# First tile of x in two banks, first norm weights in a tile of their own, two turns of attention probabilities later, last output block in half banks

## The chip, the cores and the metric

The kernel runs on one core of one Trainium2 chip. The metric is the device time of one execution in microseconds (us), the median of several runs. TensorE is called PE here, VectorE DVE, ScalarE ACT, GpSimd POOL and SyncE SP. PSUM is the memory that PE writes its results to, in banks of 512 float32 columns on 128 partitions, and SBUF is the memory that holds all other tiles.

## What is computed

Two layers on x of 512 tokens by 1024 columns, float32. Each layer is, cut to what matters:

```python
h = rmsnorm(x, norm_mix)
z = h @ w_in                      # q, k, v of attention, q, k, v, o and gates of the mLSTM, two branch gates
att = sliding_window_attention(q_a, k_a, v_a, att_sinks)
hm = sigmoid(o_m) * rmsnorm(mlstm_chunkwise(q_m, k_m, v_m, i_pre, f_pre))
mixed = sigmoid(g_a) * (att @ w_att_branch) + sigmoid(g_m) * (hm @ w_m_branch)
x = x + mixed @ w_out
u = relu(rmsnorm(x, norm_ffn) @ w_ff1)
x = x + (u * u) @ w_ff2
```

Attention has 8 query heads on 2 key heads and works on blocks of 128 queries, each of which sees its own block and the one before.

## The kernel before

x stays in SBUF for the whole program, in four tiles `xtok[t][j]` of 2 x 128 tokens by 512 columns. A product needs columns of x as rows, so PE turns x in pieces of 128 columns (`Norm.transposes`, four 128x128 transposes into one bank), and ACT and DVE scale the piece by the norm weight and split it into a high part and a rest (`Norm.turn`, `split`). Weights are loaded by SP, 512 columns at a time, and split in the same way (`chunk`): ACT writes the high part `wh`, DVE the rest `wl`. Each product of a 128-row piece is then three matmuls (`mm3`, line 203): high by high, high by rest, rest by high. Every one of them is recorded on line 47, and every transpose on line 52.

**The order of the work** is written by hand. `weave` (line 255) takes a list of steps with widths (0.25 is one `mm3` group), and puts side jobs between them at the places that numbers name. On each engine the instructions then stand in one fixed order, and an instruction waits for the semaphores of what it reads and of what last used its buffer. PSUM is given out in turn: the three banks of the tag `aux` go round, so the fourth request waits until the readers of the first are done.

**The start** (lines 357 to 399). SP and ACT each ask for one half of the first 128 columns of x (line 373), ACT then for the first 256 norm weights as a column (`gain0`, line 380), for all weights of both layers as rows (`grow`, line 381) and for its half of the next 128 columns of x. PE runs dummy matmuls on ones until data is there, turns the first piece of x into one bank (`x0`, line 393), turns `grow` (line 395), runs three more dummy matmuls (line 398), and begins with the products of the first piece: four with `wh` and the high part, four with `wl`, four with the rest. The four differ in the 128 tokens that they take from the turned piece. Between the first two fours stands the turn of the second piece of x. `turn_first` (line 310) has ACT make the high part of the first piece (line 313), and DVE makes its rest between the first two weight splits (lines 172 to 178, 316). The turned norm weights are copied to `gcol` by DVE (line 175), and the pieces of x from the third on are scaled by `gcol`.

**Attention** is woven into the gate products of each layer. There are eight units (128 queries, one key head), numbered i = 0 to 7. For each, lines 936 to 943 place the scores (`att_scores`, two banks of aux), the softmax, the turn of the probabilities (`att_probs`: PE transposes into aux, ACT and DVE split it, POOL masks it) and the product with the values (`att_out`, one bank of aux, read by ACT line 744 and DVE line 748). `turn_at` on line 938 says when the probabilities are turned.

**The end.** The second product of the MLP of the last layer ends with slot 4 of its last part (`product`, line 1619, with `which` = "aux"). It adds up 256 tokens by 512 columns in two banks of aux, in two halves h of two 128-row pieces each; in h = 1 the first block's products stand before those of the second. `gain` (line 1316) has DVE scale each block and add it to x (line 1327), the last block in two halves of 256 columns, and SP and ACT write them out (line 1330).

Of the kernel before, what the change touches and what calls it, by code (L numbers as in the profile page):

```python
# [8 lines left out]
F32 = mybir.dt.float32  # L9
# [4 lines left out]
ALU = mybir.AluOpType  # L14
# [19 lines left out]
def hybrid_kernel(ctx, tc, x, norm_mix, w_in, att_q_norm, att_k_norm, att_sinks, m_gate_bias,  # L34
# [69 lines left out]
    def f32(ap):  # L104
        return ap.bitcast(F32)
# [16 lines left out]
    neg = const.tile([MH, P], F32, name="neg")  # L122
    gp.memset(neg, NEG)
    grow = const.tile([24, P], F32, name="grow")
    gcol = const.tile([P, 40], F32, name="gcol")

    first_gains = []

    def gains(row, c0, held=False):
        n = row.shape[0]  # L130
        gps = aux([P, n])
        pe.transpose(gps, row, ident[:n, :n])
        if held:
            first_gains.append((gcol[:, c0:c0 + n], gps))
        else:
            ve.tensor_copy(gcol[:, c0:c0 + n], gps)

    def g_mix(l, k):
        return gcol[:, 8 * l + k:8 * l + k + 1]
# [10 lines left out]
    def chunk(src, behind=()):  # L150

        with tc.high_priority():
            raw = now["wraw"].tile([P, T], F32, tag="w", name=nm("w"))
            off = 0
            for s in src:
                n = s.shape[1]
                if first_loads:

                    n0 = {0: 0, 1: 2}.get(chunks[0], len(first_loads) - 1)
                    with tc.issue_after(first_loads[n0].ins):  # L160
                        first_weights.append(nc.sync.dma_start(raw[:, off:off + n], s))
                    chunks[0] += 1
                    if chunks[0] == 8:
                        first_loads.clear()
                else:
                    asked[0] = nc.sync.dma_start(raw[:, off:off + n], s)
                off += n
        with tc.high_priority(lead[0]):
            wh = now["wsp"].tile([P, T], F32R, tag="wh", name=nm("wh"))
            wl = now["wsp"].tile([P, T], F32R, tag="wl", name=nm("wl"))  # L170
            n = chunks[0] - 1 if first_loads else KT
            if n == 0 and first_rest:
                made = ve.tensor_copy(wh[:, :off], raw[:, :off])
                for then in (lambda: ve.tensor_tensor(wl[:, :off], raw[:, :off], f32(wh[:, :off]), op=ALU.subtract),
                             first_rest.pop(), lambda: ve.tensor_copy(*first_gains.pop())):
                    with tc.issue_after(made.ins):
                        made = then()
                return wh, wl
            with ExitStack() as order:
                for i in behind:  # L180
                    order.enter_context(tc.issue_after(i.ins))
                if n < KT:

                    order.enter_context(tc.issue_after(norm0.hi[max(n - 1, 0)].ins))
                    order.enter_context(tc.issue_after(norm0.lo[max(n - 1, 0)].ins))
                sc.activation(wh[:, :off], raw[:, :off], AF.Copy)  # L186
                ve.tensor_tensor(wl[:, :off], raw[:, :off], f32(wh[:, :off]), op=ALU.subtract)  # L187
        return wh, wl
# [90 lines left out]
    class Norm:  # L279
# [30 lines left out]
        def turn_first(self, ps):  # L310
            self.groups[0] = [inp.tile([P, 4, T], F32R, tag=t, name=nm("i")) for t in ("ih", "il")]
            h, lo = self.acts[0] = [g[:, 0, :] for g in self.groups[0]]
            self.hi[0] = last_split[0] = sc.activation(h, ps, AF.Copy, scale=self.gain(0))

            def rest():
                self.lo[0] = last_split[1] = made = ve.scalar_tensor_tensor(lo, ps, self.gain(0), f32(h), op0=ALU.mult,
                                                                            op1=ALU.subtract)
                return made

            first_rest.append(rest)  # L320

# [55 lines left out]
    with tc.high_priority():  # L377
        load_x(0, 1, 0, nc.sync)
        load_x(0, 1, 1, nc.scalar)
        nc.scalar.dma_start(gain0, norm_mix[0, 0:2 * P].rearrange("(k p) -> p k", p=P))  # L380
        nc.scalar.dma_start(grow[0:16, :], norm_mix.rearrange("l (k p) -> (l k) p", p=P))
# [61 lines left out]
    def mixer(l, norm, late, order, phase):  # L443
# [791 lines left out]
    def mlp(l, norm, phase):  # L1235
# [80 lines left out]
        def gain(t, j, ps, done=False, last=False):  # L1316

            with tc.high_priority():  # L1320
                for i in range(2):
                    b = 2 * t + i
                    xh = xtok[t][j][:, i, :]

                    for c in ((0, H), (H, T)) if done and last and b == NB - 1 else ((0, T),):
                        cc = slice(*c)
                        ve.scalar_tensor_tensor(xh[:, cc], ps[i][:, cc], ms[j][:, b:b + 1], xh[:, cc],  # L1327
                                                op0=ALU.mult, op1=ALU.add)
                        if done and final:
                            (nc.scalar if c[0] else nc.sync).dma_start(  # L1330
                                out[0, b * P:(b + 1) * P, j * T + c[0]:j * T + c[1]], xh[:, cc])
# [287 lines left out]
        def product(which, fresh, w, sources, gains, seeds=None):  # L1619
# [12 lines left out]

            def run(h):
                if h == 0 and fresh:
                    pairs[which] = [aux(), aux()] if which == "aux" else two_banks(which)
                ps, (hi, lo), (ah, al) = pairs[which], ws[h], a[0]
                at = [(kt, i) for kt in range(2 * h, 2 * h + 2) for i in range(2)]

                for kt, i in sorted(at, key=lambda e: e[1]) if h else at:
                    c = slice(i * P, (i + 1) * P)  # L1640
                    mm3(ps[i], ah[:, kt, c], al[:, kt, c], hi[:, kt % 2, :], lo[:, kt % 2, :],
                        fresh and kt == 0, False, skip_group_check=True)

            def done():
                for t, j, d in gains:
                    gain(t, j, pairs[which], d, which == "aux")
# [241 lines left out]
```

## Time and profile before

| what | value |
|---|---|
| median of 3 runs | 1263.53 us (1263.24 to 1263.57) |
| the profiled execution's own time | 1263.76 us |
| span of that execution, first to last instruction | 1262.1 us |
| what lies around the span | 1.66 us |
| busy time of PE, DVE, ACT, POOL | 1255.6, 1034.8, 813.3, 283.2 us |
| mean granted clock of PE | 1.000 |

A profile row of the timeline reads: start in us, length in us, engine, line, operation, tile written <- tiles read, shape, how many of a kind in a row, and in brackets how long the engine had been idle and what ended that. "ACTq" or "SPq" is the queue of an engine that issues a transfer. A matmul's length holds its way through the array, which overlaps the next one: 512 columns are shown as 0.39 us long, and the starts of two in a row lie about 0.23 us apart. The time that a matmul takes is therefore read from the distance of the starts.

### The profile page before, as it was taken

To read this page: it belongs to the slowest core of one execution; us is meant where nothing else is said; L and a number is where in the kernel's file an instruction comes from. 1 tells how busy PE (TensorE), PEld (TensorE's weight loads), DVE (VectorE), ACT (ScalarE), POOL (GpSimd) and SP (SyncE) were. 2 spreads that over 40 slices of the span, in tenths; PEclk is the share of its full clock that TensorE was granted. 3 is DMA by queue.
4 is the path that set the end of the run, shared out by engine and by line. 5 is a ranking of instruction groups with operands and counts; after the bars stand their busy time and mean duration, and the time that the engine had idled before them with its cause. 6 is when DMAs were issued, how large, how long until landed. Compare 5 with 4: busy or idle time off the path is not lost.

```text
span 1262.1 us, 19896 instructions
## 1 busy us (share of the span) xinstructions
PE 1255.6 (99%) x7170; PEld 1098.8 (87%) x7170; DVE 1034.8 (82%) x1645; ACT 813.3 (64%) x1442; POOL 283.2 (22%) x373
## 2 busy tenths in 40 slices
PE   9999999999999999999999999999999999999998
PEld 7888888888999899999888888888889999999987
DVE  5788988688998877878857989876889978778787
ACT  5578578645785665656554885876467766556563
POOL 4514131021122021031115042310303211311300
PEclk9999999999999999999999999999999999999999
DMA  5424573468899889997224354634779988998953
GB/s 159 114 69 134 127 130 93 142 137 212 179 250 182 233 170 211 235 187 190 36 75 118 89 137 110 117 111 132 156 208 189 240 191 228 171 223 207 201 134 100
DMA packets 145538, 199.68 MB, mean 158 GB/s; under 512 B 11032, under 2 KB 85632, under 8 KB 145440
## 3 DMA queue, kind: packets, MB, share of 16 engines
q0 software_dynamic: 50432, 68.30, 33.9%
q1 hardware_dynamic: 94016, 129.72, 33.5%
q8 instruction: 56, 0.92, 0.3%
q10 hardware_dynamic: 992, 0.40, 0.1%
q14 instruction: 42, 0.34, 0.1%
HBM read 195.24 MB, written 2.10 MB: 156 GB/s over the span
## 4 chain that ended last, share of the span: by engine, by line
PE 99%; DMA 0%; ACTq 0%; DVE 0%; issue 0%; DVEq 0%
PE mm L47 84%; PE aux L47 13%; PE aux L52 3%; DMA grow<-in_norm_mix_dram 0%; ACTq L373 0%; ACTq L380 0%; DVE x L1327 0%; DVEq L1884 0%
## 5 line engine op out<-in xcount | busy, mean ns | idle before, releaser
L1263 ACT ACTIVATE wh<-raw 128x1024 fp32r<-128x1024 f32 x224 | 235.0, 1055 | 149.9 <-PE mm L47 75.9
L1264 DVE TENSOR_TENSOR wl<-raw,wh 128x1024 fp32r<-128x1024 f32 x224 | 271.3, 1221 | 73.5 <-ACT wh L1263 70.7
L47 PE MATMUL mm<-i,wh 128*128 128x256 f32 (+1 forms) x1344 | 331.1, 339 | 0.0
L47 PEld LDWEIGHTS mm<-i,wh 128*128 128x128 f32 x1344 | 223.8, 190 | 19.4
L47 PE MATMUL mm<-i,wl 128*128 128x256 f32 (+1 forms) x672 | 224.7, 335 | 0.0
L47 PE MATMUL mm<-wh,uh 128*128 128x512 f32 x440 | 172.1, 391 | 0.0
L47 PE MATMUL mm<-wl,uh 128*128 128x512 f32 x440 | 171.7, 390 | 0.0
L47 PE MATMUL mm<-wh,ul 128*128 128x512 f32 x440 | 171.3, 389 | 0.0
L1425 POOL DMA_DIRECT2D raw<-in_w_ff_dram x56 | 72.5, 1375 | 349.3 <-DVE wl L1264 85.4
L47 PEld LDWEIGHTS mm<-i,wl 128*128 128x128 f32 x672 | 127.4, 190 | 13.5
L186 ACT ACTIVATE wh<-w 128x512 fp32r<-128x512 f32 (+1 forms) x143 | 85.3, 603 | 60.9 <-PE mm L47 44.0
L187 DVE TENSOR_TENSOR wl<-w,wh 128x512 fp32r<-128x512 f32 (+1 forms) x143 | 95.5, 671 | 34.8 <-ACT wh L186 34.0
L47 PE MATMUL mm<-t,wh 128*128 128x256 f32 x576 | 104.5, 283 | 0.0
L47 PE MATMUL mm<-wh,i 128*128 128x512 f32 (+1 forms) x352 | 99.5, 357 | 0.0
L47 PEld LDWEIGHTS mm<-wh,ul 128*128 128x128 f32 x440 | 82.6, 188 | 17.5
L47 PEld LDWEIGHTS mm<-wh,uh 128*128 128x128 f32 x440 | 82.8, 188 | 16.2
L47 PEld LDWEIGHTS mm<-wl,uh 128*128 128x128 f32 x440 | 82.8, 188 | 15.5
L47 PEld LDWEIGHTS mm<-t,wh 128*128 128x128 f32 x576 | 90.7, 192 | 1.3
L1674 POOL DMA_DIRECT2D raw<-in_w_ff_dram x40 | 48.4, 1214 | 169.8 <-DVE wl L1264 120.7
L47 PE MATMUL mm<-t,wl 128*128 128x256 f32 x288 | 81.5, 283 | 0.0
L1327 DVE SCALAR_TENSOR_TENSOR x<-mm,ms,x 128x512 f32<-128x512 f32 x102 | 72.4, 745 | 10.7 <-PE mm L47 10.4
L47 PEld LDWEIGHTS mm<-wh,i 128*128 128x128 f32 x352 | 62.0, 188 | 8.6
(336 smaller groups left out, 2536.6 us busy)
## 6 DMA issues: line engine op xcount, KB each, us to landing
raw<-in_w_ff_dram SPq DMA_DIRECT2D x144, 512.0 KB, 6.0
raw<-in_w_ff_dram POOLq DMA_DIRECT2D x96, 512.0 KB, 7.8
w<-in_w_in_dram SPq DMA_DIRECT2D x112, 256.0 KB, 2.8
a<-in_w_in_dram POOLq DMA_DIRECT2D x32, 256.0 KB, 5.7
qa<-in_w_out_dram POOLq DMA_DIRECT2D x12, 512.0 KB, 6.0
a<-in_w_in_dram SPq DMA_DIRECT2D x16, 256.0 KB, 4.4
w<-in_w_att_branch_dram SPq DMA_DIRECT2D x16, 256.0 KB, 3.1
w<-in_w_m_branch_dram SPq DMA_DIRECT2D x16, 256.0 KB, 2.7
```

What stands on the lines that cost most here:

```text
L47: latest[0] = nc.tensor.matmul(*args, **kw)
L52: latest[0] = nc.tensor.transpose(*args)
L186: sc.activation(wh[:, :off], raw[:, :off], AF.Copy)
L187: ve.tensor_tensor(wl[:, :off], raw[:, :off], f32(wh[:, :off]), op=ALU.subtract)
L1263: last_high[0] = sc.activation(hi, src, AF.Copy)
L1264: last_rest[0] = ve.tensor_tensor(lo, src, f32(hi), op=ALU.subtract)
L1327: ve.scalar_tensor_tensor(xh[:, cc], ps[i][:, cc], ms[j][:, b:b + 1], xh[:, cc], op0=ALU.mult, op1=ALU.add)
L1425: return gp.dma_start(to[h], src(h, i, j), accum_op=ALU.add)
L1674: gp.dma_start(to[h], src(h, i, j), accum_op=ALU.add)
```

## The change

It has four parts, and nothing else in the order of the engines moves.

1. The first turned piece of x goes to two aux tiles of 256 columns, each for two blocks of tokens. ACT makes the high part in two instructions and DVE the rest in two.
2. The rows of `norm_mix` go to a tile of their own, `grow0`, and are turned later: `gains_behind` places the transpose behind the products with `wl`, and DVE copies the result to `gcol` at once, where before the copy was held back for a place of its own. One dummy matmul stands ahead of the products, where there were three.
3. The turn of the probabilities moves by 0.25 for unit 4 (from +0.25 to +0.5) and for unit 5 (from 0 to +0.25), in both layers.
4. The last output block is added up in two tiles of 256 columns, half a bank of aux and half of the pair "y". Each of its 12 matmuls of 512 columns becomes two of 256, in h = 1 all of the first half ahead of the second.

```diff
+    grow0 = const.tile([16, P], F32, name="grow0")
...
-                made = ve.tensor_copy(wh[:, :off], raw[:, :off])
-                for then in (lambda: ve.tensor_tensor(wl[:, :off], raw[:, :off], f32(wh[:, :off]), op=ALU.subtract),
-                             first_rest.pop(), lambda: ve.tensor_copy(*first_gains.pop())):
-                    with tc.issue_after(made.ins):
-                        made = then()
+                high = ve.tensor_copy(wh[:, :off], raw[:, :off])
+                with tc.issue_after(high.ins):
+                    low = ve.tensor_tensor(wl[:, :off], raw[:, :off], f32(wh[:, :off]), op=ALU.subtract)
+                with tc.issue_after(low.ins):
+                    first_rest.pop()()
...
+            cs = [slice(2 * P * t, 2 * P * (t + 1)) for t in range(2)]
+            for c, ps in zip(cs, halves):
+                self.hi[0] = last_split[0] = sc.activation(h[:, c], ps, AF.Copy, scale=self.gain(0))
...
-            x0 = norm.transposes(0)
-        with tc.issue_after(latest[0].ins):
-            gains(grow[0:16, :], 0, True)
-        with tc.issue_after(latest[0].ins):
-            for _ in range(3):
-                pe.matmul(idle[:, :P], ones, ones, start=True, stop=True)
+            x0 = [aux((P, 2 * P)) for _ in range(2)]
+            for b in range(NB):
+                pe.transpose(x0[b // 2][:, b % 2 * P:(b % 2 + 1) * P], xtok[b // 2][0][:, b % 2, 0:P], ident)
+        with tc.issue_after(latest[0].ins):
+            pe.matmul(idle[:, :P], ones, ones, start=True, stop=True)
...
-            turn_at = at + 3.45 + (0.25 if i == 4 else 0)
+            turn_at = at + 3.45 + {4: 0.5, 5: 0.25}.get(i, 0)
...
-                    pairs[which] = [aux(), aux()] if which == "aux" else two_banks(which)
+                    pairs[which] = ([aux(), [aux((P, H)), banks("y")[:, 0, :H]]] if which == "aux"
+                                    else two_banks(which))
...
-    late = ([(max(0.25, k - 0.85), lambda k=k: turn_behind(norm, k)) for k in range(1, KT)]
+    late = ([(0.6, gains_behind)] + [(max(0.25, k - 0.85), lambda k=k: turn_behind(norm, k)) for k in range(1, KT)]
```

On PE at the start of the program, before the change (`x_0` are the two tiles that hold the first columns of x, `i` the split pieces of x, `aux` the banks that go round):

```order
L52 MATMUL aux_105<-ident,x_0_86 128x128 x2
L52 MATMUL aux_105<-ident,x_0_88 128x128 x2
L52 MATMUL aux_110<-ident,grow 128x16
L47 MATMUL aux_101<-ones 128x128 x3
L47 MATMUL mm_178<-wh_184,i_115 128x512
L47 MATMUL mm_179<-wh_184,i_115 128x512
L47 MATMUL mm_180<-wh_184,i_115 128x512
L47 MATMUL mm_181<-wh_184,i_115 128x512
L52 MATMUL aux_194<-ident,x_0_86 128x128 x2
L52 MATMUL aux_194<-ident,x_0_88 128x128 x2
L47 MATMUL mm_178<-wl_185,i_115 128x512
```

The same place after the change, from the last dummy matmul to the first product with the rest of the first piece:

```order
L47 MATMUL aux_102<-ones 128x128
L47 MATMUL mm_177<-wh_183,i_113 128x512
L47 MATMUL mm_178<-wh_183,i_113 128x512
L47 MATMUL mm_179<-wh_183,i_113 128x512
L47 MATMUL mm_180<-wh_183,i_113 128x512
L52 MATMUL aux_193<-ident,x_0_87 128x128 x2
L52 MATMUL aux_193<-ident,x_0_89 128x128 x2
L47 MATMUL mm_177<-wl_184,i_113 128x512
L47 MATMUL mm_178<-wl_184,i_113 128x512
L47 MATMUL mm_179<-wl_184,i_113 128x512
L47 MATMUL mm_180<-wl_184,i_113 128x512
L52 MATMUL aux_204<-ident,grow_84 128x16
```

The turn of the norm weights has moved from ahead of the first product to behind the eighth; the turn of the second piece of x stands where it stood.

On DVE at the start, after the change, from the rest of the first piece to that of the third (`gcol` are the turned norm weights):

```order
L315 SCALAR_TENSOR_TENSOR i_114<-aux_106,gain_1_91,i_113 128x256
L315 SCALAR_TENSOR_TENSOR i_114<-aux_107,gain_1_91,i_113 128x256
L183 TENSOR_TENSOR wl_214<-w_211,wh_213 128x512
L196 SCALAR_TENSOR_TENSOR i_114<-aux_193,gain_1_91,i_113 128x512
L183 TENSOR_TENSOR wl_239<-w_236,wh_238 128x512
L132 COPY gcol<-aux_204 128x16
L196 SCALAR_TENSOR_TENSOR i_114<-aux_220,gcol,i_113 128x512
```

The copy to `gcol` stood behind the first `wl` of this list before, and now stands behind the second, directly ahead of the third piece of x, whose scale it is.

On PE in the attention of the first layer, after the change (`kT,tq` are scores, `ident,t` turns of probabilities, `t,v` products with the values, all in aux; the rows of gate products between them are left out where "..." stands):

```order
L47 MATMUL aux_1417<-kT_637,tq_647 128x256 x4
...
L52 MATMUL aux_1430<-ident,t_1205 128x128 x4
L47 MATMUL aux_1445<-t_1318,v_116_639 128x512
...
L47 MATMUL aux_1474<-kT_637,tq_647 128x256 x4
...
L47 MATMUL aux_1502<-kT_637,tq_647 128x256 x4
L52 MATMUL aux_1509<-ident,t_1302 128x128 x4
```

Unit 4's turn (`t_1205`) stood one group of three gate products earlier and now stands directly ahead of unit 3's product with the values; unit 5's turn (`t_1302`) stood ahead of the last scores of this list and now stands behind them, so it takes the next bank in the round, the one that holds unit 3's product with the values.

More of the change, by code (lines that the diff above doesn't have):

```diff
@@ L132, in gains @@
         pe.transpose(gps, row, ident[:n, :n])
[L133 to L136, printed above, removed]
+        ve.tensor_copy(gcol[:, c0:c0 + n], gps)
     def g_mix(l, k):
@@ L308, in turn, with turn_first @@
             self.hi[k], self.lo[k] = last_split
-        def turn_first(self, ps):
+        def turn_first(self, halves):
             self.groups[0] = [inp.tile([P, 4, T], F32R, tag=t, name=nm("i")) for t in ("ih", "il")]
             h, lo = self.acts[0] = [g[:, 0, :] for g in self.groups[0]]
-            self.hi[0] = last_split[0] = sc.activation(h, ps, AF.Copy, scale=self.gain(0))
+            cs = [slice(2 * P * t, 2 * P * (t + 1)) for t in range(2)]
+            for c, ps in zip(cs, halves):
+                self.hi[0] = last_split[0] = sc.activation(h[:, c], ps, AF.Copy, scale=self.gain(0))
             def rest():
-                self.lo[0] = last_split[1] = made = ve.scalar_tensor_tensor(lo, ps, self.gain(0), f32(h), op0=ALU.mult,
-                                                                            op1=ALU.subtract)
-                return made
+                for c, ps in zip(cs, halves):
+                    self.lo[0] = last_split[1] = ve.scalar_tensor_tensor(lo[:, c], ps, self.gain(0), f32(h[:, c]),
+                                                                         op0=ALU.mult, op1=ALU.subtract)
             first_rest.append(rest)
@@ L1314, in neither, with gain @@
                 ve.scalar_tensor_tensor(d, p, -1.0, q, op0=ALU.mult, op1=ALU.subtract)
-        def gain(t, j, ps, done=False, last=False):
+        def gain(t, j, ps, done=False):
             with tc.high_priority():
@@ L1323, in gain @@
                     xh = xtok[t][j][:, i, :]
[L1325 removed]
+                    halved = isinstance(ps[i], list)
+                    for c in ((0, H), (H, T)) if halved else ((0, T),):
                         cc = slice(*c)
[L1327 to L1328 removed]
+                        ve.scalar_tensor_tensor(xh[:, cc], ps[i][c[0] // H] if halved else ps[i], ms[j][:, b:b + 1],
+                                                xh[:, cc], op0=ALU.mult, op1=ALU.add)
                         if done and final:
@@ L1645, in done @@
                 for t, j, d in gains:
-                    gain(t, j, pairs[which], d, which == "aux")
+                    gain(t, j, pairs[which], d)
                 if seeds:
```

15 lines of the change are left out of this document (9 added, 6 removed).

## Prediction

> **What bounds the kernel now.** The first page says that PE is busy nearly throughout:
>
> ```profile
> PE 1255.6 (99%) x7170; PEld 1098.8 (87%) x7170; DVE 1034.8 (82%) x1645; ACT 813.3 (64%) x1442; POOL 283.2 (22%) x373
> ```
>
> The waits of PE name two places, and the second is one that the change touches:
>
> ```profile
> PE aux L47 <- POOL ones L114: 1.2, 1, 1.2
> PE aux L52 <- DMA grow<-in_norm_mix_dram: 0.8, 1, 0.8
> ```
>
> So all that an edit can win is distance between matmuls that is longer than it need be: 1262.1 - 1255.6 = 6.5 us idle, 2.0 of them in these two waits, and what hides inside "busy". I therefore read the timeline at the places of the change. A change of 0.2% (2.5 us) is about what a measurement of this kernel can tell from none.
>
> The start on PE, then on ACT with its queue, then the transfers that were asked for there:
>
> ```profile
> 3.94 1.03 PE L52 MATMUL aux<-ident,x 128*128 128x128 f32 x4
> 5.96 0.94 PE L47 MATMUL aux<-ones 128*128 128x128 f32 x6
> 6.65 1.18 PE L47 MATMUL mm<-wh,i 128*128 128x512 f32 x4
> 7.67 0.60 PE L52 MATMUL aux<-ident,x 128*128 128x128 f32 x4
> 8.02 1.18 PE L47 MATMUL mm<-wl,i 128*128 128x512 f32 x4
> ```
>
> ```profile
> 1.35 0.49 ACTq L380 DMA_DIRECT2D gain<-in_norm_mix_dram  x1
> 2.39 0.45 ACTq L373 DMA_DIRECT2D x<-in_x_dram  x1
> 5.01 0.69 ACT L313 ACTIVATE i<-aux,gain 128x512 fp32r<-128x512 f32 x1 [0.86 <-PE aux L52]
> ```
>
> ```profile
> gain<-in_norm_mix_dram ACTq DMA_DIRECT2D x1, 1.0 KB, 3.5
> x<-in_x_dram ACTq DMA_DIRECT2D x1, 128.0 KB, 4.8
> ```
>
> ACT has the high part at 5.01 + 0.69 = 5.70, but PE sits behind `grow` and the dummies until 6.65. That is the wait that goes. What is late next is in the last row: half of the second piece of x, asked for at 2.39, lands at 2.39 + 4.8 = 7.19. Today its transposes start at 7.67 and never meet it.
>
> **Part 1 and 2, the start.** The scale lands at 1.35 + 3.5 = 4.85, so ACT's first half of the high part runs from about 4.9 to 5.3 and the second to about 5.75; two halves are no faster than one whole, but the products of the first two token blocks can begin at about 5.4. Four products take 7.67 - 6.65 = 1.02, so they end at about 6.4. Then the second pair of transposes waits for 7.19. Whatever the bank split brings forward, this wait takes back: with one whole tile the products would run from 5.75 to 6.8 and wait for the same 7.19, so I cost the split itself at nothing. Its extra instructions on ACT and DVE lie in the idle time before the second weights.
>
> Today the products with `wl` start 8.02 - 7.67 = 0.35 after the first of four transposes, half of which, 0.17, belongs to the second pair. So they start at 7.19 + 0.17 = 7.36 instead of 8.02: 0.66 earlier. Then comes the turn of the norm weights, which used to lie in the wait. Its price is read from the other turn of this kind, later on PE:
>
> ```profile
> 27.33 0.40 PE L47 MATMUL mm<-wl,i 128*128 128x512 f32 x1
> 27.56 0.40 PE L47 MATMUL mm<-wh,i 128*128 128x512 f32 x1
> 27.89 0.24 PE L52 MATMUL aux<-ident,grow 24*128 24x24 f32 x1
> ...
> 28.39 0.40 PE L47 MATMUL mm<-wl,i 128*128 128x512 f32 x1
> ```
>
> From 27.56 to 28.39 are 0.83, where two products alone take 2 x 0.23: the turn costs 0.37. Left over at the start: 0.66 - 0.37 = **0.29**. Its low end is nothing or a loss of 0.1, if the piece of x lands 0.3 to 0.4 later than here; its high end is set by the next thing that could be late, the third piece:
>
> ```profile
> 8.30 0.17 DVE L175 COPY gcol<-aux 128x16 f32<-128x16 f32 x1
> 10.59 0.69 DVE L187 TENSOR_TENSOR wl<-w,wh 128x512 fp32r<-128x512 f32 x1 [0.81 <-ACT wh L186]
> 11.29 0.69 ACT L199 ACTIVATE i<-aux,gcol 128x512 fp32r<-128x512 f32 x1 [0.73 <-DVE wl L187]
> 12.01 0.75 DVE L200 SCALAR_TENSOR_TENSOR i<-aux,gcol,i 128x512 fp32r<-128x512 f32 x1 [0.73 <-ACT i L199]
> 13.61 0.39 PE L47 MATMUL mm<-wh,i 128*128 128x512 f32 x1
> ```
>
> The copy to `gcol` now stands on DVE behind the `wl` that ends at 11.28, and ACT's 11.29 waits for it: both move by 0.2, and the rest of the third piece, which ended at 12.76, ends at 12.96. PE reads it first at 13.61, so 0.6 is the most that the start can win. With 0.29 the cover holds. Behind DVE's copy stand that rest and the next `wl`, each 0.2 later, and their readers have the same cover.
>
> **Part 3, the turns of probabilities.** In each layer one turn starts late: 0.50 after the matmul before it, where the next turn in the same layer starts 0.23 after.
>
> ```profile
> 104.61 0.39 PE L47 MATMUL mm<-i,wl 128*128 128x512 f32 x1
> 105.11 0.63 PE L52 MATMUL aux<-ident,t 128*128 128x128 f32 x4
> 109.30 0.64 PE L47 MATMUL aux<-kT,tq 128*128 128x256 f32 x4
> 109.77 0.63 PE L47 MATMUL mm<-i,wh 128*128 128x512 f32 x2
> 110.24 0.39 PE L47 MATMUL mm<-i,wl 128*128 128x512 f32 x1
> 110.47 0.63 PE L52 MATMUL aux<-ident,t 128*128 128x128 f32 x4
> 729.81 0.39 PE L47 MATMUL mm<-i,wl 128*128 128x512 f32 x1
> 730.31 0.63 PE L52 MATMUL aux<-ident,t 128*128 128x128 f32 x4
> ```
>
> ```profile
> 103.51 0.69 DVE L716 TENSOR_TENSOR t<-t,den 128x512 f32<-128x512 f32 x1
> 104.12 0.84 DVE L748 TENSOR_TENSOR t<-aux,t 64x256 f32<-64x256 f32 x2
> 110.25 0.84 DVE L748 TENSOR_TENSOR t<-aux,t 64x256 f32<-64x256 f32 x2
> ```
>
> Unit 4's probabilities are ready at 104.20, so what PE waits for is its bank: DVE leaves unit 2's product with the values at 104.96, 0.15 before the turn starts. One group of three products later (0.70 from 109.77 to 110.47) PE comes at 105.11 - 0.27 + 0.70 = 105.54 and finds it free. That gives 0.27 per layer, **0.54** in both.
>
> Unit 5 pays with a new wait. Its turn now takes the bank of unit 3's product with the values, which DVE leaves at 111.09, usable at 111.24. PE gets there at 109.03 (109.30 - 0.27), plus 0.47 for those scores, two groups at 0.70 and 0.47 for the last scores: 111.37. The cover is 0.13. If it is gone, up to 0.27 per layer comes back; the range of this part is 0 to 0.54. The later masks on POOL and the later splits are read by products with the values some 2 us later, and cost nothing.
>
> **Part 4, the last block.** Products of 512 and of 256 columns, 24 and 48 in a row, from the chain, then the end on PE, DVE and ACT's queue, and a single 256-wide addition from the groups:
>
> ```profile
> 1163.66 5.47 PE mm L47 x24
> 1169.13 5.75 PE aux L47 x48
> ```
>
> ```profile
> 1257.48 0.39 PE L47 MATMUL aux<-wh,ul 128*128 128x512 f32 x1
> 1257.90 0.88 DVE L1327 SCALAR_TENSOR_TENSOR x<-aux,ms,x 128x256 f32<-128x256 f32 x2 [0.61 <-PE aux L47]
> 1258.81 0.37 ACTq L1330 DMA_DIRECT2D out_dram<-x  x1
> ```
>
> ```profile
> L1362 DVE SCALAR_TENSOR_TENSOR x<-aux,gcol,x 128x256 f32<-128x256 f32 x8 | 3.6, 477 | 0.0
> ```
>
> 12 products at 5.47/24 = 0.228 become 24 at 5.75/48 = 0.120: 2.88 - 2.74 = 0.14 more. In return the first half is complete 6 x 0.12 = 0.72 before the end, longer than the 0.48 that DVE needs for it, and only one addition follows the last matmul: 0.88 - 0.48 = 0.40 less. Net **0.26** earlier for ACT's output, which is the last to be asked for; between 0.1 (if the two halves' transfers get in each other's way) and 0.35.
>
> The Trainium skill speaks against this part ("Perfetto Trace Analysis", Optimizing Tensor Performance: larger matmuls are the more efficient), and its formula for the spacing ("TensorE: Matmul & The Clock Gate", Back-to-back issue gap) has 2.5 ns for each matmul more; by that, an estimate, the halving would cost 12 x 2.5 ns = 0.03 instead of 0.14; the rows here show the larger price, and the sum goes by them.
>
> **The sum.** 0.29 + 0.54 + 0.26 = 1.09 us earlier. The profiled execution's own time is 1263.76 (span 1262.1 and 1.66 around it), which would become 1262.67; it lies 0.23 above the median of 1263.53, so for the median I say **1262.4**.
>
> **The rivals.**
> 1. *The wait for x takes the place of the wait for `grow`, in full.* If the second piece lands at 7.48 or later, the start wins nothing: 1262.7. For it: the row is one transfer among several in flight. Against: today's runs agree within 0.33.
> 2. *Unit 5's wait takes the place of unit 4's.* A cover of 0.13 is gone if DVE's chain to 111.09 is no faster than here while PE is earlier: 0 instead of 0.54, time 1263.0.
> 3. *Slower: PE's clock stays low for longer.* Four transposes take 1.03 at 3.94 and 0.60 at 7.67, and the dummies at 5.96 lie between: PE begins at about half speed and has sped up by 7.67. The change removes dummies and puts two holes (about 0.35 and 0.8 us) into the first 7 us. If the slow phase then lasted to the end of the first twelve products, the eight after 7.19 would take 0.23 more each and the transposes 0.43 more: 2.3 lost, with 0.8 won in parts 3 and 4 and 0.29 at the start, time 1264.7. It decides at whether the products at 7.36 stand 0.23 or 0.46 apart. Against: today a hole of 0.8 at the same place does no harm, and real products start earlier than the dummies did. The Trainium skill ("TensorE: Matmul & The Clock Gate", Part 1) has the clock rise after a busy window of about 3.4 us and fall only after an idle one; by that rule no hole here is long enough.
> 4. *More.* If x lands earlier, the start wins up to 0.6: 1262.1.
>
> That the edits don't do what they say is excluded for the order of the engines; that the two-bank tile by itself moves nothing is part of the forecast.
>
> **How the numbers follow.** Forecast 0.62, rival 1 0.12, rival 2 0.12, rival 3 0.06, rival 4 0.08. The range takes in the low ends of parts 1 to 4 and rivals 1, 2 and 4, with the runs' spread of 0.3 at both ends: 1261.8 to 1263.4. No case but an unnamed one passes 2.5 us either way: even all parts at their best give 0.6 + 0.54 + 0.35 = 1.5. So faster by over 0.2% 0.02, within 0.95, slower 0.03.
>
> **What would show it.** Right: the first product at about 5.4, the second transposes split by a wait until 7.2, the `wl` products from 7.36 and those of the second piece 0.3 earlier than before; unit 4's and 5's turns 0.23 behind the matmul before them in both layers; one addition of 0.48 behind the last matmul. Wrong: a turn with 0.4 or more ahead of it; products 0.46 apart behind 7 us; a hole ahead of the third piece's products at about 12.8; an end that is not 0.26 nearer to the last matmul.

## The result and the profile after

| kernel | runs | median (us) | lowest to highest |
|---|---|---|---|
| before | 17 | 1263.82 | 1263.24 to 1265.86 |
| after | 17 | 1266.40 | 1265.00 to 1269.96 |
| before, on a later chip | 15 | 1265.22 | 1263.34 to 1265.98 |
| after, on that chip | 11 | 1264.70 | 1263.26 to 1268.46 |

The ratio is 1.0018 [1.0011, 1.0026] in the first set and 1.0001 [0.9992, 1.0010] in the second. So the change cost 2.6 us or nothing, and did not win the 1.1 us that I forecast: 1266.4 lies outside my range (1261.8 to 1263.4).

The runs of before fall into two groups. Of 125 in five sets, 65 lie between 1262.99 and 1264.36 and 60 between 1264.74 and 1266.24; the three that I saw ahead of the prediction were all of the lower group. What parts them, by the profiles below, is how soon PE's clock rises at the start, so single profiles are compared here by places and not by their end.

The profiled execution of after took 1268.20 (span 1266.5) and is one of the longest. The first line of its page says that PE's busy time has grown by 1.8 us, so that most of the 4.4 us of span are not in PE's work:

```profile
PE 1257.4 (99%) x7178; PEld 1098.6 (87%) x7178; DVE 1033.1 (82%) x1646; ACT 813.1 (64%) x1443; POOL 284.5 (22%) x373
```

All waits of PE in it (waited for; us in total, times, longest):

```profile
PE mm L47 <- ACT wh L182: 2.0, 2, 1.6
PE aux L47 <- POOL ones L114: 1.2, 1, 1.2
PE mm L47 <- ACT i L311: 0.6, 1, 0.6
PE mm L47 <- ACT kvi L463: 0.6, 1, 0.6
PE mm L47 <- DVE wl L183: 0.5, 2, 0.2
```

The wait for `grow` is gone. New at the start is a wait of the first product for ACT's high part (`i`). The other new ones are for weight splits (`wh`, `wl`) and for `kvi` (a product that ACT copies out of PSUM), and none of them is at a place that the change touches.

**The three places of the change.** The start and the third piece of x, on PE:

```profile
3.94 0.66 PE L52 MATMUL aux<-ident,x 128*128 128x128 f32 x4
...
5.42 1.20 PE L47 MATMUL mm<-wh,i 128*128 128x512 f32 x4 [0.60 <-ACT i L311]
6.46 0.88 PE L52 MATMUL aux<-ident,x 128*128 128x128 f32 x4
7.09 1.17 PE L47 MATMUL mm<-wl,i 128*128 128x512 f32 x4
8.20 0.23 PE L52 MATMUL aux<-ident,grow 16*128 16x16 f32 x1
...
13.31 0.51 PE L47 MATMUL mm<-wh,i 128*128 128x512 f32 x1
13.65 0.60 PE L52 MATMUL aux<-ident,x 128*128 128x128 f32 x4
```

The first product stands at 5.42 (6.65 before), the `wl` products at 7.09 (8.02 before), the next transposes at 13.65 (13.85 before): 0.20 won. The turns of units 4 and 5 in the first layer, each with the row ahead of it:

```profile
106.06 0.40 PE L47 MATMUL mm<-i,wl 128*128 128x512 f32 x1
106.29 0.60 PE L52 MATMUL aux<-ident,t 128*128 128x128 f32 x4
...
111.60 0.63 PE L47 MATMUL aux<-kT,tq 128*128 128x256 f32 x4
112.20 0.63 PE L52 MATMUL aux<-ident,t 128*128 128x128 f32 x4
```

Unit 4's turn starts 0.23 behind the matmul ahead of it (0.50 before). Unit 5's stands behind four scores, which take 4 x 0.12 = 0.48, and starts 0.60 after the first of them: it waits 0.12. The end:

```profile
1262.42 0.28 PE L47 MATMUL mm<-wh,ul 128*128 128x256 f32 x1
1262.74 0.48 DVE L1325 SCALAR_TENSOR_TENSOR x<-mm,ms,x 128x256 f32<-128x256 f32 x1 [0.23 <-PE mm L47]
1263.26 0.37 ACTq L1328 DMA_DIRECT2D out_dram<-x  x1
```

One addition of 0.48 follows the last matmul, as forecast.

**Where the time went.** The same matmul can be found in both timelines; the difference of its two starts says how far PE is behind before at that place (13.65 - 13.85 = -0.20). It changes at these places only:

| place in after (us) | what happens there | PE behind before, from then on |
|---|---|---|
| 0 to 14 | the start | -0.20 |
| 44.5 | wait for `kvi`, whose ACT stood behind a late weight split | +0.67 |
| 84 | a chance wait of a turn | +0.75 |
| 106 to 112 | turns of units 4 and 5 | +0.53 |
| 149 to 150 | wait for DVE, weights late since 142 | +1.12 |
| 170 to 172 | wait for `wh`, then `wl` | +2.48 |
| 733 to 739 | turns of units 4 and 5 | +2.25 |
| 797 to 800 | wait for `wh`, then `wl` | +4.77 |
| 870 | a chance wait that before had | +4.66 |
| end | last block | +4.44 |

The places of the change won 0.20 + 0.22 + 0.23 + 0.22 = 0.87 together; the four other waits lost 0.87 + 0.59 + 1.36 + 2.52 = 5.3. The first of them, on ACT and on PE:

```profile
43.79 1.31 ACT L182 ACTIVATE wh<-w 128x512 fp32r<-128x512 f32 x2 [2.25 <-DMA w<-in_w_in_dram]
45.01 1.58 ACT L463 ACTIVATE kvi<-mm,ncol 128x264 f32<-128x264 f32 x4
45.52 0.74 PE L47 MATMUL mm<-i,wh 128*128 128x512 f32 x2 [0.60 <-ACT kvi L463]
```

In before the same copies of ACT stand at 44.27 and PE does not wait for them:

```profile
44.27 1.58 ACT L466 ACTIVATE kvi<-mm,ncol 128x264 f32<-128x264 f32 x4
```

The largest, on ACT and on PE:

```profile
798.15 0.63 ACT L182 ACTIVATE wh<-w 128x512 fp32r<-128x512 f32 x1 [4.29 <-DMA w<-in_w_in_dram]
798.83 0.50 PE L47 MATMUL mm<-wh,i 128*128 128x512 f32 x1 [1.61 <-ACT wh L182]
```

ACT stood idle for 4.29 us until a weight load landed, and PE for the split behind it. What is different ahead of that load is found on POOL: a cast of 64x512 (before line 774, after line 771; it copies half of a split mLSTM query to other partitions), behind which POOL issues loads that add gate weights onto a tile (`a`, line 817). First before, POOL and then DVE beside it:

```profile
778.00 2.34 POOL L774 CAST a<-a 64x512 fp32r<-64x512 f32 x1 [25.25 <-ACT a L772]
780.29 0.86 POOL L817 DMA_DIRECT2D a<-in_w_in_dram  x1
```

```profile
779.21 0.65 DVE L197 TENSOR_TENSOR t<-sc,t 128x512 fp32r<-128x512 f32 x1
779.97 0.92 DVE L823 TENSOR_TENSOR wl<-a,wh 128x512 fp32r<-128x512 f32 x1
```

Then after:

```profile
780.69 4.15 POOL L771 CAST a<-a 64x512 fp32r<-64x512 f32 x1 [24.75 <-ACT a L769]
784.79 0.86 POOL L814 DMA_DIRECT2D a<-in_w_in_dram  x1
```

```profile
781.90 0.65 DVE L193 TENSOR_TENSOR t<-sc,t 128x512 fp32r<-128x512 f32 x1
782.49 0.67 DVE L820 TENSOR_TENSOR wl<-a,wh 128x512 fp32r<-128x512 f32 x1
783.09 0.14 DVE L531 TENSOR_TENSOR mp<-t,gr 4x1 f32<-4x1 f32 x1
783.16 1.20 DVE L864 SCALAR_TENSOR_TENSOR sc<-sc,i 128x1024 f32<-128x1024 f32 x1
```

Before, DVE has a hole of 0.1 at 779.9; the cast ends 0.48 behind the start of that hole (780.34), and DVE's next instruction takes 0.92 instead of 0.67. After, DVE's instructions follow each other without a hole there, and the cast ends only at 784.84, again 0.48 behind the end of a DVE instruction (783.16 + 1.20 = 784.36). POOL's load stands at 784.79 instead of 780.29, 4.5 later, where PE is 2.25 behind. SP's next three weight loads now meet more of these loads. KB and median us to landing, from 787 to 791.5 before and from 789 to 794 after:

```profile
w<-in_w_in_dram SPq DMA_DIRECT2D x3, 256.0 KB, 4.3
```

```profile
w<-in_w_in_dram SPq DMA_DIRECT2D x3, 256.0 KB, 6.9
```

### The profile page after: what moved, and what is told of

Read it like the earlier page. It is cut to its first block, busy times and chain, and to the rows that moved or that the text cites. A ratio compares the mean times of both kernels' runs of the same rounds, so it can differ in the third digit from the quotient of the medians.

```text
span 1266.5 us, 19914 instructions
## 1 busy us (share of the span) xinstructions
PE 1257.4 (99%) x7178; PEld 1098.6 (87%) x7178; DVE 1033.1 (82%) x1646; ACT 813.1 (64%) x1443; POOL 284.5 (22%) x373
## 4 chain that ended last, share of the span: by engine, by line
PE 92%; DMA 3%; DVE 3%; ACT 2%; issue 0%; ACTq 0%; DVEq 0%; SPq 0%
PE mm L47 78%; PE aux L47 12%; PE aux L52 2%; DMA w<-in_w_in_dram 2%; DVE wl L183 1%; ACT wh L182 1%; DMA w<-in_w_att_branch_dram 0%; DVE t L345 0%; DMA gain<-in_norm_mix_dram 0%; DVE p L1013 0%; ACT t L708 0%; ACT tq L667 0%; DVE p L792 0%; DVE wl L820 0%; DVE t L745 0%
## 5 line engine op out<-in xcount | busy, mean ns | idle before, releaser
L47 PE MATMUL mm<-wh,uh 128*128 128x512 f32 (+1 forms) x444 | 173.1, 390 | 0.0
L47 PE MATMUL mm<-wl,uh 128*128 128x512 f32 (+1 forms) x444 | 172.8, 389 | 0.0
L47 PE MATMUL mm<-wh,ul 128*128 128x512 f32 (+1 forms) x444 | 172.3, 388 | 0.0
L1325 DVE SCALAR_TENSOR_TENSOR x<-mm,ms,x 128x512 f32<-128x512 f32 (+1 forms) x103 | 72.8, 742 | 10.0 <-PE mm L47 9.3
```

The costliest lines, as they stand in the source:

```text
L47: latest[0] = nc.tensor.matmul(*args, **kw)
L1325: ve.scalar_tensor_tensor(xh[:, cc], ps[i][c[0] // H] if halved else ps[i], ms[j][:, b:b + 1], xh[:, cc], op0=ALU.mult, op1=ALU.add)
```

## The experiments

Theory A is this chain: later turns, DVE later against PE, a cast that finds no hole, late loads of gate weights, late weights, PE waits. Theory B was the start with its new tile. Theory C came with the first four runs: PE's code is loaded in pieces of 16 KB, and the start, which has eight PE instructions fewer (two matmuls, each recorded twice, with as many weight loads), moves these loads onto weight loads.

**Which part loses?** The later turns alone, on the kernel before:

```diff
-            turn_at = at + 3.45 + (0.25 if i == 4 else 0)
+            turn_at = at + 3.45 + {4: 0.5, 5: 0.25}.get(i, 0)
```

> The kernel before with the later turns of probabilities for units 4 and 5 alone. In the trace of the changed kernel every local gain that was forecast is there, but PE waits for weights in the mLSTM part, 1.1 us at about 171 and 2.3 us at about 797, behind a cast of POOL that took 4.15 us instead of 2.34. Theory A: the later turns leave VectorE later against PE, POOL's cast then meets a closed run of VectorE's work, its loads of gate weights go out about 2 us later and crowd the next weight loads. Then this kernel is slower than before by about 2 us (2 x 0.25 won, 1 to 2.3 lost at each of the two places), its two casts take over 4 us, and PE waits for wh behind them. Theory B: it is the start (0.2 us earlier, and a new tile of 512 bytes on each partition that moves the addresses of all later tiles). Then this kernel is 0.4 to 0.5 us faster than before, and the casts take 2.3.

Measured: 1265.49 (1262.82 to 1266.64), ratio 1.0002 [0.9993, 1.0011], so the total tells nothing. The profile does: both casts take 4.1, and PE falls back by 0.84 at about 169 and by 1.5 at about 795, with 0.23 and 0.21 won at the turns. Nothing is lost at 44.5. Theory A holds for these two places.

The counterpart, after with the old places of the turns:

```diff
-            turn_at = at + 3.45 + {4: 0.5, 5: 0.25}.get(i, 0)
+            turn_at = at + 3.45 + (0.25 if i == 4 else 0)
```

> The changed kernel with the old places of the turns of units 4 and 5; start and last block as changed. Theory A: the casts take about 2.3 us, no wait for wh at 171 or 797, and the time is that of before less 0.4 (0.19 at the start, 0.22 at the end), unless the wait of 0.77 us at about 44.5, ahead of the later turns in the program, belongs to the start: then it is 0.4 slower than before. Theory B: 2 to 3 us slower than before, with the waits in place.

Measured: 1264.00 (1263.13 to 1265.54), ratio 1.0000 [0.9991, 1.0009]. The wait at 44.5 is there (0.48), so it belongs to the start; there is none at 797, where the cast took 2.33. In the first layer the cast took 4.12 even so, and 0.28 was lost: a long cast doesn't need the turns. Theory B, which had 2 to 3 us for this kernel, falls.

One unit at a time, on the kernel before:

```diff
+            turn_at = at + 3.45 + (0.5 if i == 4 else 0)
```

> The kernel before with the turn of unit 4 alone 0.25 later. Theory A, if it is unit 4's later turn that costs: 1.5 to 2.5 us slower, casts over 4 us. If it is unit 5's: 0.4 to 0.5 us faster (two turns start 0.25 us sooner behind the matmul ahead of them). Theory B: 0.4 to 0.5 us faster.

```diff
+            turn_at = at + 3.45 + (0.25 if i in (4, 5) else 0)
```

> The kernel before with the turn of unit 5 alone 0.25 later. Theory A, if it is unit 5's later turn that costs: 2 to 3 us slower, casts over 4 us; unit 4's turn still waits 0.5 behind the matmul ahead of it. If it is unit 4's: within 0.3 us of before. Theory B: within 0.3 us of before.

Measured: 1264.14 (1263.54 to 1266.16), ratio 1.0003 [0.9994, 1.0011], and 1265.18 (1263.18 to 1268.35), ratio 1.0006 [0.9997, 1.0015]. All four casts took 2.3, so neither single turn is shown to be the cause. With unit 4 alone PE loses about 0.25 in each layer instead of winning it, since unit 5's turn then waits (it starts 0.79 and 0.75 behind the matmul ahead of it). The profile of unit 4 alone also showed something else, at the start, which is the same as that of before:

```profile
5.72 0.28 PE L52 MATMUL aux<-ident,grow 16*128 16x16 f32 x1 [0.72 <-DMA grow<-in_norm_mix_dram]
5.93 1.65 PE L47 MATMUL aux<-ones 128*128 128x128 f32 x6
7.24 2.05 PE L47 MATMUL mm<-wh,i 128*128 128x512 f32 x4
9.09 0.85 PE L52 MATMUL aux<-ident,x 128*128 128x128 f32 x4
```

Four products take 9.09 - 7.24 = 1.85 instead of 1.02, and PE is 1.66 late from there on. The six rows of dummies take 1.65 where they took 0.94: in the profile of before the clock has risen by the time that PE comes out of its wait for `grow`, at 5.8, and here it rises only at about 9.5 (the transposes behind 9.09 are still 0.21 apart, and 0.11 in before).

**The cast.** After, with the first of the four casts in each layer replaced by a memset, all engines in the same order:

```diff
-                gp.tensor_copy(d[o], f32(d[r]))
+                if m or i:
+                    gp.tensor_copy(d[o], f32(d[r]))
+                else:
+                    gp.memset(f32(d[o]), 0.0)
```

> The changed kernel with the first of POOL's four casts in each layer (the one that took 4.1 us) replaced by a memset that waits for nothing; the copied half of that tile is left out. All engines keep their order. Theory A (the cast, and the loads of gate weights behind it, push the next weight loads): the waits for wh at about 171 and 797 go; 1266.4 becomes about 1264.2, and only the wait of 0.6 to 0.9 us at about 44.5 is left. Theory C (the start takes eight matmul and weight-load instructions away, so PE's code loads of 16 KB come later and cross weight loads): no change, 1266.

Measured: 1262.98 (1262.48 to 1264.18), ratio to before 0.9986 [0.9977, 0.9996]. No wait at 171 or 797 is left, and the one at 44.5 is (0.46). It is faster than the 1264.2 that I had for it: against the kernel with both edits (below) the wait at 44.5 is worth 0.4 in the median.

The opposite, before with the first cast done four times, so that the second to fourth load of gate weights go out later:

```diff
-                gp.tensor_copy(d[o], f32(d[r]))
+                for _ in range(1 if m or i else 4):
+                    gp.tensor_copy(d[o], f32(d[r]))
```

> The kernel before with POOL's first cast of each layer done four times, three of them behind the first load of gate weights, so that POOL's next loads of gate weights are issued about 2 us later; nothing else is moved. Theory A: the weight loads that follow land late, PE waits for wh at about 168 and 795, and the time is 1.5 to 2.5 us longer. Theory C: within 0.3 us of before.

Measured: 1264.95 (1263.56 to 1267.53), ratio 1.0007 [0.9999, 1.0016]. The profile has the late clock (1.66) and then falls back by 0.22 in the first layer and 1.0 at 797, without any later turn. Late loads of gate weights alone make PE wait, by less than expected.

**The code loads.** After, with as many dummies as before had:

```diff
-            pe.matmul(idle[:, :P], ones, ones, start=True, stop=True)
+            for _ in range(3):
+                pe.matmul(idle[:, :P], ones, ones, start=True, stop=True)
```

> The changed kernel with three dummy matmuls at the start where it has one, so that PE has as many instructions ahead of the first product as before; they lie in its wait of 0.6 us for ScalarE and cost nothing there. Theory C: PE's code load near 40 is back at 40.1 or earlier, measured against PE's work, and the wait of 0.6 to 0.9 us at about 44.5 is gone: about 1265.5. Theory A alone: 44.5 is an accident of the loads or of the earlier start, and the time stays at 1266.4.

Measured: 1264.02 (1262.24 to 1264.73), ratio 0.9996 [0.9987, 1.0005]. The wait at 44.5 is gone, and the median is 1.5 below the 1265.5 that I expected; behind a cast of 4.13 in the first layer PE loses 1.1 from 169 on, behind one of 2.33 in the second nothing. The opposite is before with two dummies fewer:

```diff
-            for _ in range(3):
-                pe.matmul(idle[:, :P], ones, ones, start=True, stop=True)
+            pe.matmul(idle[:, :P], ones, ones, start=True, stop=True)
```

> The kernel before with one dummy matmul behind the turn of the norm weights instead of three: eight PE instructions fewer ahead of the first product, nothing else. Theory C: the products start 0.3 to 0.5 us sooner, PE's code load near 40 moves back by about 0.5 us against PE's work, and a wait of 0.4 to 0.8 us appears at about 44.5; the time is that of before within 0.5. If there is no such wait, the code load is not its cause, or not alone. The late rise of PE's clock (9.1 instead of 6.1 us in some executions, 1.7 us each) should stay, as the hole ahead of the turn of the norm weights stays: runs in two groups 2 us apart.

Measured: 1263.82 (1262.98 to 1266.32), ratio 0.9998 [0.9989, 1.0007]. PE is 0.69 ahead from the start and loses 0.9 at 44.1; both terms are a little larger than forecast. The two groups that I expected to stay are not plain in 11 runs: seven reach up to 1264.45, four lie from 1265.00 to 1266.32. The transfers from 39 to 43.8 us, after and then after with three dummies (code loads are the queue "instruction"; share of 16 engines; KB, median us to landing):

```profile
q8 instruction: 1, 0.02, 2.2%
issues: line engine op xcount, KB each, median us to landing
w<-in_w_in_dram SPq DMA_DIRECT2D x3, 256.0 KB, 4.1
```

```profile
q8 instruction: 1, 0.02, 1.2%
issues: line engine op xcount, KB each, median us to landing
w<-in_w_in_dram SPq DMA_DIRECT2D x3, 256.0 KB, 3.0
```

One code load lies in each. It takes 0.022 x 16 x 4.8 = 1.7 us of one engine in after and 0.9 with three dummies, and the weight loads beside it land after 4.1 and 3.0 us. Its length does not part the profiles: it is 0.96 in after with the old turns and 0.95 in before with one dummy, and PE waits in both. Its place does: with PE's lead or lag against before taken off, it starts at 39.6 to 40.3 us in the nine profiles without the wait and at 40.4 to 41.4 in the five with it. The weight load that is issued at 39.1 to 39.2 by the same count lands after 4.4 to 4.8 us in these five, and after 3.0 to 3.6 in the others.

**Both together**, three dummies and the memset:

```diff
+            for _ in range(3):
+                pe.matmul(idle[:, :P], ones, ones, start=True, stop=True)
...
+                    gp.memset(f32(d[o]), 0.0)
```

> Both of these together, on the changed kernel: three dummies, and the first cast of each layer replaced by a memset (the copied half left out). If A and C are the two causes, all that is left are the local gains of 0.86 (0.19 start, 0.22 and 0.23 attention, 0.22 end): about 1262.6, and no wait of PE over 0.3 us behind 10 us. If something else costs (the moved addresses of the tiles, say), it stays above 1264.

Measured: 1262.60 (1262.25 to 1263.05), ratio 0.9985 [0.9976, 0.9994]; the list of PE's waits holds only the one for `ones`. That is the expected number, and 0.2 from the prediction, in part by luck. Its profile is 1.16 shorter than that of before: 0.05 at the start, 0.24 and 0.23 at the turns and 0.20 at the end, 0.72 in all, and the rest elsewhere, most of it at 84 and 870, where waits come and go that the change does not touch. And the runs of before beside it have both groups (median 1264.09), of which this kernel shows only one.

**A version that leaves nothing out.** After with three dummies, and the first cast of each layer done by ACT:

```diff
+                else:
+                    sc.activation(d[o], t[r], AF.Copy)
```

> The changed kernel with three dummies, and the first of POOL's four casts in each layer done by ScalarE instead, from the unsplit tile; nothing is left out. Theory A and C together: POOL's loads of gate weights no longer stand behind a cast that meets VectorE, no wait for weights over 0.3 us, about 1262.6 like the kernel that leaves this copy out; ScalarE's 0.62 more lies in its idle time. If ScalarE's own copies are late by it, the wait moves to the scores of the mLSTM and the time is 1263.5 or more.

Measured: 1262.67 (1262.18 to 1263.45), ratio 0.9987 [0.9978, 0.9996]: faster than before and than after (1266.40 and 1264.70, on other chips). Its waits of PE, all of them:

```profile
PE aux L47 <- POOL ones L114: 1.2, 1, 1.2
```

**The start by itself**, with three dummies, the old turns and the new last block:

```diff
+            for _ in range(3):
+                pe.matmul(idle[:, :P], ones, ones, start=True, stop=True)
...
+            turn_at = at + 3.45 + (0.25 if i == 4 else 0)
```

> The changed kernel with three dummies and the old places of the turns: the new start and the new last block alone. If the new start also takes away the late rise of PE's clock, all runs lie in one group, from about 1262.9 to 1263.8 (0.22 at the end and 0 to 0.2 at the start less than the lower group of before, 1263.4), with none at 1265. If the two groups belong to the program as such, some runs lie 2 us higher. By theory A a long cast may still come now and then, as it did once with the old turns.

Measured: 1263.26 (1262.68 to 1263.84), ratio 0.9989 [0.9980, 0.9998]. One group, none at 1265, though 14 of the 27 runs of before beside it lie above 1264.7. No late rise of the clock shows with this new start.

**After once more**, with no edit:

> The changed kernel once more, unchanged, for a second profile. Taken alone, the long casts cost 1.4 (1264.02 against 1262.60 with three dummies) and the later code loads 0.4 (1262.98 against 1262.60 without the first cast); together that would be 1264.4, where 1266.4 was measured. If the two work on each other, this profile has casts over 4 us in both layers, a wait at about 44.5, and at 797 a wait of 2 us or more with PE's code load within 3 us of it (it lay at 785 to 787 in the kernels with as many PE instructions as before), and the median is again about 1266. If 1266.4 was an accident of the first chip, the median is 1264.0 to 1264.8.

Measured: 1264.70, as in the table at the top. The profiled execution, 1268.46, has all four waits again (0.73 at 44.6, then 149, 171, and 2.4 at 797, with PE's code load at 795.8), but the median is 0.3 above 1264.4, the plain sum of the two causes. The waits come together in some executions and not in others.

Over all profiles (the wait at 44.5 is the excess of one distance between matmuls over 0.23; casts are the first of each layer):

| kernel | PE instructions at the start | turns later | wait at 44.5 | casts (us) |
|---|---|---|---|---|
| before | as before | no | none | 2.32, 2.34 |
| after | fewer | 4 and 5 | 0.77 | 4.13, 4.15 |
| after once more | fewer | 4 and 5 | 0.73 | 4.13, 4.14 |
| turns alone | as before | 4 and 5 | none | 4.12, 4.13 |
| after, old turns | fewer | no | 0.48 | 4.12, 2.33 |
| unit 4 alone | as before | 4 | none | 2.32, 2.33 |
| unit 5 alone | as before | 5 | none | 2.31, 2.33 |
| after, memset | fewer | 4 and 5 | 0.46 | left out |
| after, three dummies | as before | 4 and 5 | none | 4.13, 2.33 |
| both | as before | 4 and 5 | none | left out |
| before, four casts | as before | no | none | 2.33, 2.33 |
| ACT's cast | as before | 4 and 5 | none | on ACT |
| before, one dummy | fewer | no | 0.81 | 2.33, 2.34 |
| start by itself | as before | no | none | 2.33, 2.33 |

The wait at 44.5 is in 5 of 5 profiles with fewer instructions and in 0 of 9 without. Of the casts, 7 of 8 took over 4 us with both turns later, and 1 of 14 without.

What parts all 22 casts is how late they start against PE (the cast's start less PE's lead or lag, less the cast's start in before). The 14 short ones are 0 to 0.19 later than in before, the 8 long ones 0.36 to 1.29. The hole on DVE goes with it: it is 0.10 where the cast is as early as in before, about 0 where the cast is 0.1 later, and closed (the next row starts 0.07 before the end of the one ahead) from 0.19 on. One short cast, in the second layer of after with three dummies, came through with the hole closed. The one long cast without the later turns, in after with the old turns, is 0.42 late.

## Why the prediction was wrong, step by step

**What bounds the kernel** was right but read too narrowly. PE is busy almost throughout, so each edit was weighed by PE's rows at its own place. How much time the weights have in hand 40 or 60 us further on was not looked at.

**Parts 1 and 2.** 0.29 forecast, 0.20 measured in the profile of after. The first product (5.4) and the price of the turn of the norm weights (0.37: from the fourth `wl` product to the second product behind the turn are 0.81, where I had 0.83) were right. The second piece of x landed early enough for its transposes to go on at 6.9 instead of 7.19, which gave 0.55 by 12.4; the third piece took 0.35 of it back, 0.23 in a hole at 12.9, a mark that I had named for "wrong", and 0.1 in the rows behind it. Its weights came 0.3 later than in before, so that the copy to `gcol` ended at 11.69: the cap was not 0.6 but 0.3. And 0.20 is one profile: over the eight with the new start PE is between 0.21 ahead of before and 0.21 behind it at 14 us, which goes with the time at which the clock rises. A gain of 0.29 at the start is not shown.

The step that failed here is one that wasn't made. The two dummies were removed at no price at all, and PE's instructions were counted as time only. They are also code, and by the experiments their number at the start decides whether PE waits at 44.5. That the code load is what carries this is argued from its place beside the weight loads; it was not moved by itself.

**Part 3.** 0.54 forecast, 0.45 measured: 0.27 for unit 4's turn was right, and unit 5's turn pays about 0.05 net for its bank, so rival 2 came true in a small part. The step that failed is the sentence "The later masks on POOL and the later splits are read by products with the values some 2 us later, and cost nothing." PE does not wait for them there. But DVE and ACT carry the shift on, and some 40 us later it decides whether a cast of POOL takes 2.3 or 4.1 us, and with it when the weights land. Shown are the link from the cast to the waits (the memset and ACT's copy take them away) and that the long cast comes with both turns later in 7 of 8 cases, and with a late start against PE in 8 of 8. That DVE's hole is the means is read from the traces alone, with one cast against it.

The Trainium skill ("SBUF — State Buffer", Who interferes with whom) has the rule that I needed: an instruction of VectorE with two inputs in SBUF contends with one of GpSimd that reads SBUF, the port pair that they share is an exclusive lock, and the order of issue decides which of them waits. The rows at 778 and 781 agree in that the cast ends 0.48 behind the end of such an instruction, and that the one that it gets ahead of takes 0.25 longer. Why the cast does not end sooner, beside the DVE instruction at 781.51 that takes one input from PSUM, no run shows.

**Part 4.** 0.26 forecast, 0.22 measured. Right, with its mechanism.

**The rivals.** Rival 1 did not come, and rival 4 only to 12.4. Rival 3, the clock, had its place right and its sign wrong: the late rise exists (1.7 us), but it is the old start that falls into it, in 2 of its 6 profiles and, by the two groups, in about half of its executions, and the new one in none of its 8 profiles. That the old start's hole ahead of the turn of `grow` is the reason was not tested by itself; the profile of before has one of 0.82 and no late rise, that of unit 4 alone one of 0.72 and the late rise. I had read three runs that agreed within 0.33 as the spread of the kernel. The Trainium skill's rule ("TensorE: Matmul & The Clock Gate", Part 1: a busy window of about 3.4 us, free-running) agrees with the rises under the new start, which are spread over 3.3 us, from 4.0 to 7.4; my conclusion from it, that no hole here is long enough, did not hold for the old start, whose late rises lie at 9.5 to 9.6.

**The sum and the range.** The terms of the sum were 1.09 and came out at 0.87 in the profile of after, and without the two causes the kernel stands at 1262.60 and 1262.67. The range failed because each bound in it was local; "no case but an unnamed one passes 2.5 us either way" named the gap and gave it 0.03.

Left open is why the four waits come together in more executions of the first set (none under 1265.0) than of the second, and why the last wait is 2.5 in after and 1.5 with the turns alone. PE's code load lies at 795.6 in the one and at 787.5 in the other, but no run moved it there by itself. Open too is the wait at 149, which stands in both profiles of the whole change and in no other: the three weight loads ahead of it land after 4.4 to 4.7 us (2.6 to 3.2 in before), with a code load at 141.5 and 142.5 (138.5 in before). No run separates it from the other waits.

## What to carry to other kernels

When a kernel's main engine is 99% busy, an edit's price lies also in the slack of its loads further on: follow the helper engines that the edit shifts to the next place where they share something, and ask how late the loads behind it may be. An engine's idle dummies are instructions to be loaded as well as time; when they go, look for new waits behind them. Time a kernel often enough to see whether its runs form one group or two before taking a spread from three of them.

## What the hardware showed that was not expected

- A cast of 64x512 on POOL took 0.61 us at its quickest, beside a DVE instruction that takes one input from PSUM (787.63 in after), and 2.3 or 4.1 us among DVE instructions of 0.65 to 1.2 us that mostly take both from SBUF.
- With the old start PE's clock had risen by 5.6 to 5.8 us, behind PE's wait for `grow`, in four profiles and rose at 9.5 to 9.6 us in two, with the new one between 4.0 and 7.4 us in eight (read from the distances of the first matmuls): no execution of the three best kernels (33 runs, 1262.18 to 1263.84) shows the 2 us between the groups.
- Code loads are visible work: 56 packets of 16 KB, about one for 256 of PE's 14,356 instructions (that they are PE's is read from this count), each 0.9 to 1.7 us long in the profile of after, on one of the 16 engines.
